# Two transformer-like blocks in one fp32 kernel: the experts' values taken from the second half on, seven pairs of split weights, and a skewed end

## The chip, the core and the metric

The program runs on one core of a Trainium2 chip. The metric is the device time of one execution in microseconds (us). TensorE (PE) does the matrix products, VectorE (DVE) and ScalarE (ACT) the elementwise work, GpSimd (POOL) a little of it, and SyncE (SP) issues the transfers, all on one queue.

## What is computed

256 tokens of width 1024 go through two blocks, all in float32. What matters here, cut from the reference:

```python
# first block
x = x + gt_mix * (concat([y_conv, y_rwkv]) @ w_out)
u = modulate(rmsnorm(x, norm_ffn_g), sh_ffn, sc_ffn)
x = x + gt_ffn * peer_ffn(u, w_q, sub_keys, expert_u, expert_v)
#   peer_ffn: per token 8 heads x top 16 of 16384 experts:
#   h = gelu(einsum('thkd,td->thk', expert_u[expert], u));  einsum('thk,thkd->td', gate * h, expert_v[expert])
x = rmsnorm(x, final_g)
# second block
h = rms_norm(x, g_mix_norm) * (1 + sc_m) + sh_m
q_a, k_a, v_a, q_i, k_i, w_i, q_b, k_b, v_b, gate_a, gate_b = split(h @ w_in)
merged = sigmoid(gate_a) * (dsa_attention(...) @ w_br_dsa) + sigmoid(gate_b) * (moba_attention(...) @ w_br_moba)
x = x + gt_m * (merged @ w_out)
h = rms_norm(x, g_ffn_norm) * (1 + sc_f) + sh_f
g_ff, u_ff = split(h @ w_gate_up)
x = x + gt_f * ((silu(g_ff) * u_ff) @ w_down)
```

The gates `gt_m` and `gt_f` are vectors over the 1024 features.

## The kernel before

**Split products.** A float32 product is made of three passes on TensorE. `wload` (L1560) loads a weight tile of 128x1024 (512 KB) into one of three raw slots (W_wraw), casts it to its high half (W_whi, on ACT or DVE) and subtracts to get the low half (W_wlo, mostly on DVE); whi and wlo have rings of three. The other operand is split as well (chi and clo, ah and al), and the passes are hi x whi, hi x wlo, lo x whi.

**The experts' values.** The gates and activations of all 16384 experts lie in SBUF as two halves, gH0 and gH1 (64 rows j of 128 experts each; 64 KB a partition). `values` (L2514) goes through the 128 rows: it splits the row's gates to ah and al (rings of three), loads the row of `peer_v`, and issues 12 matmuls of 128x512: two token tiles t x two halves of the output x three passes. For the last three rows a bias puts t=1 after t=0. Beside the rows, `beside_values` (L2576) computes the second block's modulation, and two gate rows: `row_bcast` (L1633) turns a column vector on 128 partitions x 8 into a row, by writing it to DRAM in 1024 four-byte pieces ("row<-") and reading it back onto all partitions.

**From the values to the attention.** `run` (L2869) adds the gated values to x, tile by tile (part final0 and final1: a chain of DVE and ACT steps for two norms), which ends in Cn_xn; TensorE transposes it, ACT casts it to C_chi, DVE makes C_clo. The first product is qk0 with weights w_qka, by `tok_skew` (L2329): token tile 0 goes over all 8 weights, then tile 1 over the KEEP=3 pairs that are still in the ring, and over 5 that are loaded again. Then follow the indexer, the selection, v, qk1, the gates, the attention, the merge.

**out2 and the feed-forward.** out2 is `tok_skew` over w_out_2, with a gated add (row gtm) to x, a norm, and the product "gua" (first 8 weights of gate-up, again `tok_skew`), the rest of gate-up, w_down, and a tail with the row gtf.

**What sets the order.** The program is not written in its final order. All operations are recorded (which is why the profile shows nearly everything at L696, the recorder's line), and a planner makes one fixed order for each engine and for the queue: it takes an operation's longest path to the end, adds a number from the table PRIORITY (one for a part, method and tile) and a local bias, and uses estimated costs for each operation and transfer. SBUF is divided into regions on a left and a right side (REGIONS, L1466); a region opens when the operations of the regions that it names are done. In the second block C0, Cn, Ca and Cf follow one another on the right side.

Of the kernel before, what the change touches and what calls it, by code (L numbers as in the profile page):

```python
# [205 lines left out]
def cost(op, out, reads):  # L206
    n = _free(out)
# [22 lines left out]
    if op.eng == "DMA":  # L230
        b = P * n * 4
        return b / 358.0 - 8
# [507 lines left out]
def _real(x):  # L740
# [28 lines left out]
WHI_ANY = 1  # L769
# [3 lines left out]
VAL_BIAS = 1.45e3  # L773
HALF_BIAS = 1.45e3
# [15 lines left out]
    "add C00 tensor_tensor xres": -2000.0,  # L790
    "add C01": -500.0,
    "add C01 scalar_tensor_tensor nsc": -6000.0,
    "add C01 tensor_mul gtmp": 2500.0,
    "add E00": 35000.0,
    "add E00 tensor_mul gtmp": 82500.0,
    "add E00 tensor_tensor xres": -14000.0,
    "add E01": 3500.0,
    "add E01 scalar_tensor_tensor nsc": -36000.0,
    "add E01 tensor_mul gtmp": -56000.0,
    "add E01 tensor_tensor xres": -145500.0,  # L800
    "attend00 copy ohi": -2000.0,
    "attend00 copy pT": -12000.0,
# [7 lines left out]
    "attend01 copy ohi": -2500.0,  # L810
# [6 lines left out]
    "attend01 transpose r": 500.0,  # L817
    "attend10 matmul n": -16000.0,
    "attend10 matmul p": -2000.0,
    "attend10 reciprocal asum": 1000.0,  # L820
# [5 lines left out]
    "attend11 reciprocal asum": -31000.0,  # L826
    "attend11 scalar_tensor_tensor lg1": 1000.0,
    "attend11 tensor_mul lg1": -3000.0,
    "attend11 tensor_reduce amax": 4000.0,
    "attend11 tensor_scalar amax": -2000.0,  # L830
    "attend11 tensor_sub olo": -2500.0,
    "base": 17500.0,
    "base dma_start dram": 500.0,
    "base dma_start nblk": -13500.0,
    "base memset ublk": -16000.0,
    "base tensor_mul ublkp": -57000.0,
    "base tensor_reduce ublk": 22500.0,
    "bonus matmul m": -26500.0,
    "bonus tensor_mul av": -1000.0,
    "bonus tensor_scalar av": -4000.0,  # L840
    "consts activation cvec": 40000.0,
    "consts dma_start clevf": -1500.0,
    "consts dma_start cmask": 10000.0,
    "consts dma_start cvec": -16000.0,
    "consts dma_start lorawa": 30000.0,
    "consts dma_start xres": 2000.0,
    "consts iota pj": -125500.0,
    "consts memset bd64": -43000.0,
    "consts memset bdones": -4500.0,
# [2164 lines left out]
```

## Time and profile before

| | us |
|---|---|
| median of three runs | 1500.91 (1496.61 to 1501.64) |
| the profiled execution | 1507.02 |
| its span | 1505.2 |
| TensorE busy in it | 1432.8 (95%) |
| VectorE busy | 1258.5 (84%) |
| ScalarE busy | 511.3 (34%) |

The profile is of one execution, 6 us above the median. The chain that ended last is TensorE 72%, VectorE 14%, transfers 9%, ScalarE 3%. The core's granted TensorE clock was 0.988 of full speed on the mean.

### The profile page before, as it was taken

The numbers are of one execution on the slowest core, as the hardware profiler recorded it, in microseconds if no ns is written. First come the engines' busy times: TensorE is split into PE (matmuls) and PEld (weight loads), VectorE is DVE, ScalarE is ACT, GpSimd is POOL, SyncE is SP. The second block draws the span as 40 slices with busy tenths as digits, with TensorE's granted clock in tenths as the row PEclk, the third lists the DMA queues.
The fourth block names the chain that finished last, engine by engine and source line by source line (L and its number), as shares of the span: only waits on it lengthen the run. The fifth ranks groups of instructions, "written<-read, shape, count | busy, mean of one in ns | idle before, by whom it ended". The sixth has DMA issues, their size and how long they took to land.

```text
span 1505.2 us, 24345 instructions
## 1 busy us (share of the span) xinstructions
PE 1432.8 (95%) x9307; PEld 1252.0 (83%) x9307; DVE 1258.5 (84%) x2395; ACT 511.3 (34%) x917; POOL 97.8 (6%) x91
## 2 busy tenths in 40 slices
PE   7999898998899999999999999999889999899998
PEld 6876666998899999999877888887668899589986
DVE  5798748999999889898879999887988987876676
ACT  2501225243434333232332233322354464533210
POOL 1100000023110000000000000000322100100000
PEclk9999999999999999999999999999999999999999
DMA  9558417544453545545788888786565454765554
GB/s 378 175 148 286 134 45 232 174 153 141 153 169 125 173 154 170 174 162 173 276 258 316 291 300 302 275 287 213 186 211 184 128 166 156 223 209 182 183 184 138
DMA packets 97348, 300.46 MB, mean 200 GB/s; under 512 B 17744, under 2 KB 24528, under 8 KB 97104
## 3 DMA queue, kind: packets, MB, share of 16 engines
q1 hardware_dynamic: 97232, 298.91, 60.4%
q8 instruction: 73, 1.20, 0.3%
q14 instruction: 43, 0.35, 0.1%
HBM read 295.58 MB, written 3.29 MB: 199 GB/s over the span
## 4 chain that ended last, share of the span: by engine, by line
PE 72%; DVE 14%; DMA 9%; ACT 3%; issue 2%; SPq 0%; POOL 0%; DVEq 0%; ACTq 0%; POOLq 0%
PE bank L696 72%; DVE W_wlo L696 4%; DMA W_wraw<-in_peer_v_dram 2%; ACT W_whi L696 1%; DMA W_wraw<-in_w_gua_dram 1%; DVE W_whi L696 1%; DMA row<-A_rowcol 1%; DMA Arw_XT<-scrx 1%; DMA row<-C_rowcol 1%; DVE Ach_ZR L696 1%; DMA W_wraw<-in_w_out_dram 1%; DVE Bt_tv L696 1%; DMA W_wraw<-in_peer_u_dram 1%; DVE Bt_tix L696 1%; DVE Bt_pos L696 1%
## 5 line engine op out<-in xcount | busy, mean ns | idle before, releaser
L696 DVE TENSOR_TENSOR W_wlo<-W_wraw,W_whi 128x1024 fp32r<-128x1024 f32 x417 | 515.8, 1241 | 40.4 <-ACT W_whi L696 21.8
L696 PE MATMUL bank<-X_u2hi,W_wlo 128*128 128x256 f32 x1088 | 295.4, 287 | 8.5 <-DVE W_wlo L696 8.3
L696 ACT CAST W_whi<-W_wraw 128x1024 fp32r<-128x1024 f32 x217 | 227.6, 1050 | 222.7 <-PE bank L696 128.1
L696 PE MATMUL bank<-X_u2hi,W_whi 128*128 128x256 f32 x1088 | 296.7, 287 | 3.6 <-ACT W_whi L696 2.9
L696 PE MATMUL bank<-X_u2lo,W_whi 128*128 128x256 f32 x1088 | 293.7, 285 | 0.0
L696 DVE CAST W_whi<-W_wraw 128x1024 fp32r<-128x1024 f32 x202 | 139.5, 691 | 88.2 <-PE bank L696 60.5
L696 PEld LDWEIGHTS bank<-X_u2hi,W_wlo 128*128 128x128 f32 x1088 | 202.7, 193 | 11.2 <-DVE W_wlo L696 11.1
L696 PEld LDWEIGHTS bank<-X_u2hi,W_whi 128*128 128x128 f32 x1088 | 203.1, 193 | 5.3 <-ACT W_whi L696 4.1
L696 PEld LDWEIGHTS bank<-X_u2lo,W_whi 128*128 128x128 f32 x1088 | 202.9, 193 | 0.0
L696 PE MATMUL bank<-W_whi,A_ah 128*128 128x512 f32 x512 | 139.7, 392 | 6.6 <-DVE W_whi L696 5.6
L696 PE MATMUL bank<-W_wlo,A_ah 128*128 128x512 f32 x512 | 139.9, 392 | 0.0
L696 PE MATMUL bank<-W_whi,A_al 128*128 128x512 f32 x512 | 139.2, 391 | 0.0
L696 PEld LDWEIGHTS bank<-W_whi,A_ah 128*128 128x128 f32 x512 | 96.6, 189 | 28.0 <-issue 6.8
L696 PEld LDWEIGHTS bank<-W_wlo,A_ah 128*128 128x128 f32 x512 | 96.8, 189 | 21.0 <-DVE W_wlo L696 0.9
L696 ACT CAST A_ah<-gH_gH 128x256 fp32r<-128x256 f32 x128 | 51.2, 406 | 184.1 <-PE bank L696 177.9
L696 PEld LDWEIGHTS bank<-W_whi,A_al 128*128 128x128 f32 x512 | 96.7, 189 | 20.5
L696 PE MATMUL bank<-C_chi,W_wlo 128*128 128x256 f32 (+1 forms) x424 | 108.1, 286 | 0.8 <-DVE W_wlo L696 0.7
L696 PE MATMUL bank<-C_chi,W_whi 128*128 128x256 f32 (+1 forms) x424 | 106.6, 284 | 0.0
L696 PE MATMUL bank<-C_clo,W_whi 128*128 128x256 f32 (+1 forms) x424 | 106.2, 284 | 0.0
L696 PEld LDWEIGHTS bank<-C_chi,W_wlo 128*128 128x128 f32 (+1 forms) x424 | 75.0, 188 | 1.7 <-DVE W_wlo L696 1.4
L696 DVE SCALAR_TENSOR_TENSOR A_mraw<-A_mraw,A_cvec 128x1024 f32<-128x1024 f32 x56 | 68.3, 1220 | 8.6 <-DMA A_mraw<-in_wmodT_dram 5.8
L696 PEld LDWEIGHTS bank<-C_chi,W_whi 128*128 128x128 f32 (+1 forms) x424 | 73.6, 187 | 0.8 <-ACT Ca_sg L696 0.2
(433 smaller groups left out, 2167.9 us busy)
## 6 DMA issues: line engine op xcount, KB each, us to landing
W_wraw<-in_peer_u_dram SPq DMA_DIRECT2D x128, 512.0 KB, 3.5
W_wraw<-in_peer_v_dram SPq DMA_DIRECT2D x128, 512.0 KB, 4.6
A_mraw<-in_wmodT_dram SPq DMA_DIRECT2D x48, 512.0 KB, 5.0
W_wraw<-in_w_gu_dram SPq DMA_DIRECT2D x36, 512.0 KB, 4.0
W_wraw<-in_w_down_dram SPq DMA_DIRECT2D x22, 512.0 KB, 4.3
W_wraw<-in_w_out_dram SPq DMA_DIRECT2D x17, 512.0 KB, 4.1
W_wraw<-in_w_gate_dram SPq DMA_DIRECT2D x16, 512.0 KB, 3.6
W_wraw<-in_peer_wqa_dram SPq DMA_DIRECT2D x13, 512.0 KB, 4.3
```

The lines of the kernel that those rows point to most:

```text
L696: return getattr(eng, "tensor_copy" if meth == "copy" and e != "ACT" else meth)(*args, **kw)
```

## The change

- Costs in the planner: the latency of a transfer is put at 1900 ns instead of 950, the rate at 385 bytes per ns instead of 358, and 900 ns more for scratch tensors whose names begin with "scr". The table PRIORITY is new in nearly every line (some 550 lines of the diff).
- `values` takes the rows in the order 64 to 127, 0 to 63, so that gH1 is free after 64 rows. In its room region Wx opens, with MORE=4 further pairs of whi and wlo (xhi, xlo): `wload` goes round seven pairs, three of W and four of Wx. The raw ring stays at three.
- The last LAST=7 rows have their own ring of seven for ah and al in Wx, and a bias that puts t=1 of them 9 us later.
- qk0 runs with the seven pairs and keeps all seven, and so loads one weight again instead of five. Afterwards the three pairs of W are used, until out2, where region Wf gives four more; out2 and gua load one weight again instead of five each.
- A region Cq on the right side holds what qk0 produces and the rope's temporaries. Ca opens after Wx too. The rows gtm and gtf are in Cf, which opens after Ca and Cq, instead of C0.

```diff
-DMA_LAT = 950.0
+DMA_LAT = 1900.0
     if op.eng == "DMA":
         b = P * n * 4
-        return b / 358.0 - 8
+        small = any(x.tensor.name.startswith("scr") for x in [out] + reads)
+        return b / 385.0 + (900.0 if small else 0.0)
...
 PRIORITY = {
-    "values4 tensor_tensor wlo": 14500.0,
+    "values4 matmul o": -23000.0,
...
+    "Wx": dict(side="left", after=["gH1"], on=["A3"]),
     "C0": dict(side="right", after=["Bk", "gH0", "gH1"]),
+    "Cq": dict(side="right", after=["Bk", "gH0", "gH1"], on=["C0"]),
-    "Ca": dict(side="right", after=["Cn", "A3"]),
-    "Cf": dict(side="right", after=["Ca"]),
+    "Ca": dict(side="right", after=["Cn", "A3", "Wx"]),
+    "Cf": dict(side="right", after=["Ca", "Cq"]),
+    "Wf": dict(side="left", after=["Ca", "Cq"]),
...
     def wload(self, ap, n=1024):
+        self.turn = (self.turn + 1) % (3 + MORE) if self.more else 0
         raw = self.T("W", "wraw", [1024], F32, WRAW)[:, 0:n]
         nc.sync.dma_start(raw, ap)
-        hi = self.T("W", "whi", [1024], F32R, 3)[:, 0:n]
-        (nc.any.copy if WHI_ANY else nc.scalar.copy)(hi, raw)
-        lo = self.T("W", "wlo", [1024], F32R, 3)[:, 0:n]
+        more = self.turn >= 3
+        hi = self.T(self.more, "xhi", [1024], F32R, MORE)[:, 0:n] if more else self.T("W", "whi", [1024], F32R, 3)[:, 0:n]
+        nc.any.copy(hi, raw)
+        lo = self.T(self.more, "xlo", [1024], F32R, MORE)[:, 0:n] if more else self.T("W", "wlo", [1024], F32R, 3)[:, 0:n]
...
 def tok_skew(net, hi, lo, aps, tag):
+    keep = KEEP + MORE if net.more else KEEP
-    tok_mm(net, hi, lo, aps, ps, order_back(0), (1,), kept=kept)
+    tok_mm(net, hi, lo, aps, ps, order_back(keep), (1,), kept=kept, keep=keep)
...
     def values(self, side):
-        for j in range(128):
+        for n in range(128):
+            j = (n + 64) % 128
+            last = n >= 128 - LAST
+            if n == 64:
+                net.more = "Wx"
+            part = lambda x: net.T("Wx", x + "x", [32, 8], F32R, LAST) if last else net.T("A3", x, [32, 8], F32R, 3)
-                        nc.bias = -VAL_BIAS * (2 * t + h) if j >= 125 else 0.0
+                        nc.bias = -VAL_LATE * t - VAL_BIAS * h if last else 0.0
...
     def run(self, peer_ps, out):
+        net.more = "Wf"
-        gtm = net.row_bcast("C0", 1, 2, "row", 2, scale=0.5)
+        gtm = net.row_bcast("Cf", 1, 2, "row", 2, scale=0.5)
...
-        gtf = net.row_bcast("C0", 1, 5, "row", 2)
+        gtf = net.row_bcast("Cf", 1, 5, "row", 2)
```

TensorE at the end of the values and the start of qk0, before: bank_61 and bank_60 are tile 0's output, bank_62 and bank_63 tile 1's, A_ah and A_al a row's split gates, W_whi and W_wlo its split values.

```order
L696 MATMUL bank_62<-W_whi_85,A_ah_6965 128x512
L696 MATMUL bank_62<-W_wlo_88,A_ah_6965 128x512
L696 MATMUL bank_62<-W_whi_85,A_al_6968 128x512
L696 MATMUL bank_63<-W_whi_85,A_ah_6965 128x512
L696 MATMUL bank_63<-W_wlo_88,A_ah_6965 128x512
L696 MATMUL bank_63<-W_whi_85,A_al_6968 128x512
L696 MATMUL bank_64<-G_ident_74,Cn_xn_9305 128x128 x4
L696 MATMUL bank_65<-G_ident_74,Cn_xn_9306 128x128 x4
```

Before, the last 18 matmuls of tile 1 stand between tile 0's last one and the transposes (the last row of tile 1 is shown). After, bank_63 and bank_62 are tile 0's, bank_61 and bank_60 tile 1's:

```order
L697 MATMUL bank_62<-W_whi_86,Wx_alx_8151 128x512
L697 MATMUL bank_61<-W_whi_85,Wx_ahx_8138 128x512
L697 MATMUL bank_61<-W_wlo_88,Wx_ahx_8138 128x512
L697 MATMUL bank_61<-W_whi_85,Wx_alx_8145 128x512
L697 MATMUL bank_60<-W_whi_85,Wx_ahx_8138 128x512
L697 MATMUL bank_60<-W_wlo_88,Wx_ahx_8138 128x512
L697 MATMUL bank_60<-W_whi_85,Wx_alx_8145 128x512
...
L697 MATMUL bank_60<-W_whi_86,Wx_ahx_8144 128x512
L697 MATMUL bank_60<-W_wlo_89,Wx_ahx_8144 128x512
L697 MATMUL bank_60<-W_whi_86,Wx_alx_8151 128x512
L697 MATMUL bank_65<-G_ident_74,Cn_xn_9248 128x128 x4
L697 MATMUL bank_64<-G_ident_74,Cn_xn_9249 128x128 x4
```

Now 42 matmuls of tile 1, those of the last seven rows, stand there (the first six and the last three are shown).

The queue (SP) at the end of the values, before: C_rowcol is the column of gtm, C_row its row.

```order
L696 DMA C_rope_9273<-in_rope_dram 128x384
L696 DMA C_causal_9275<-in_causal_dram 128x128
L696 DMA row<-C_rowcol_9294 128x8x1
L696 DMA C_row_9295<-row 128x1024
L696 DMA C_row_9296<-row 128x1024
L696 DMA W_wraw_82<-in_w_qka_dram 128x1024
L696 DMA W_wraw_83<-in_w_qka_dram 128x1024
L696 DMA W_wraw_84<-in_w_qka_dram 128x1024
```

The queue in out2, after (Cf_rowcol and Cf_row the same column and rows):

```order
L697 DMA W_wraw_82<-in_w_out_dram 128x1024
L697 DMA W_wraw_84<-in_w_out_dram 128x1024
L697 DMA row<-Cf_rowcol_11064 128x8x1
L697 DMA W_wraw_83<-in_w_out_dram 128x1024
L697 DMA Cf_row_11065<-row 128x1024
L697 DMA W_wraw_82<-in_w_out_dram 128x1024
L697 DMA W_wraw_84<-in_w_out_dram 128x1024
L697 DMA Cf_row_11066<-row 128x1024
L697 DMA W_wraw_83<-in_w_out_dram 128x1024
L697 DMA W_wraw_82<-in_w_gua_dram 128x1024
```

The scatter has moved from the front of the qk0 loads to between the fifth and the sixth load of w_out; its read-back stands before the last three loads.

VectorE in out2, after: the end of the merge (Ca_mg), then the column, and the splits of out2's weights (the third to sixth of its eight).

```order
L697 SCALAR_TENSOR_TENSOR Ca_mg_0_9708<-Ca_sg_9694,bank_63 128x512
L697 TENSOR_TENSOR Ca_mg_9707<-Ca_mg_9707,Ca_mg_0_9708 128x512
L697 TENSOR_TENSOR C_clo_9215<-Ca_mg_9707,C_chi_9214 128x512
L697 TENSOR_SCALAR Cf_rowcol_11064<-G_mod_78 128x8
L697 CAST Wf_xhi_11103<-W_wraw_83 128x1024
L697 SCALAR_TENSOR_TENSOR Cf_nsc_11069<-G_mod_78,G_cols_72 128x8
L697 TENSOR_TENSOR Wf_xlo_11107<-W_wraw_83,Wf_xhi_11103 128x1024
L697 TENSOR_TENSOR Wf_xlo_11108<-W_wraw_82,Wf_xhi_11104 128x1024
L697 TENSOR_TENSOR Wf_xlo_11109<-W_wraw_84,Wf_xhi_11105 128x1024
L697 CAST Wf_xhi_11106<-W_wraw_83 128x1024
L697 TENSOR_TENSOR Wf_xlo_11110<-W_wraw_83,Wf_xhi_11106 128x1024
```

The column stands right behind the merge's last operations, ahead of the splits of the third to sixth weight.

## Rows read from the trace of the kernel before

**Rows 1.** The page's busy times: busy us, share of the span, instructions.

```profile
PE 1432.8 (95%) x9307; PEld 1252.0 (83%) x9307; DVE 1258.5 (84%) x2395; ACT 511.3 (34%) x917; POOL 97.8 (6%) x91
```

**Rows 2.** The page's costliest group: busy us, mean ns, idle before.

```profile
L696 DVE TENSOR_TENSOR W_wlo<-W_wraw,W_whi 128x1024 fp32r<-128x1024 f32 x417 | 515.8, 1241 | 40.4 <-ACT W_whi L696 21.8
```

**Rows 3.** Stretches: us; busy of PE, PEld, DVE, ACT, POOL; clock; DMA share, GB/s.

```profile
0.00:420.00 420.00, 379.37 (x2586) 318.40 (x2587) 340.80 (x931) 138.98 (x223) 46.50 (x53) 0.98 0.55 182
860.00:1000.00 140.00, 140.00 (x620) 115.83 (x619) 124.85 (x182) 48.89 (x78) 0.00 (x0) 1.00 0.86 295
1060.30:1118.30 58.00, 47.66 (x193) 35.35 (x192) 50.08 (x86) 26.80 (x53) 20.03 (x20) 0.94 0.58 188
1273.10:1332.80 59.70, 52.83 (x214) 36.24 (x213) 50.84 (x70) 30.98 (x48) 4.57 (x3) 1.00 0.70 218
```

**Rows 4.** TensorE's timeline, end of values and qk0: start, us, [idle before].

```profile
1083.74 1.67 PE L696 MATMUL bank<-G_ident,Cn_xn 128*128 128x128 f32 x8 [4.22 <-DVE Cn_xn L696]
1087.26 1.22 PE L696 MATMUL bank<-W_whi,C_chi 128*128 128x512 f32 x2 [1.85 <-ACT C_chi L696]
...
1091.51 0.63 PE L696 MATMUL bank<-W_whi,C_clo 128*128 128x512 f32 x2
1091.98 0.63 PE L696 MATMUL bank<-W_whi,C_chi 128*128 128x512 f32 x2
...
1095.94 0.73 PE L696 MATMUL bank<-W_wlo,C_chi 128*128 128x512 f32 x2 [0.54 <-DVE W_wlo L696]
...
1099.60 1.11 PE L696 MATMUL bank<-G_ident,Cn_xn 128*128 128x128 f32 x8 [1.06 <-DVE Cn_xn L696]
```

**Rows 5.** VectorE's timeline at the same place.

```profile
1074.31 0.69 DVE L696 TENSOR_TENSOR A_mraw<-bank,A_gtf 128x512 f32<-128x512 f32 x1 [0.52 <-PE bank L696]
...
1083.14 1.15 DVE L696 TENSOR_SCALAR Cn_xn<-A_mraw,A_f2r,A_f2t 128x512 f32<-128x512 f32 x2
```

**Rows 6.** The queue's timeline at the same place.

```profile
1074.66 0.43 SPq L696 DMA_DIRECT2D row<-C_rowcol  x1
1086.36 0.80 SPq L696 DMA_DIRECT2D C_row<-row  x2
```

**Rows 7.** Transfers, 160 to 185 and 770 to 790: KB, us to landing.

```profile
row<-G_mod SPq DMA_DIRECT2D x1, 4.0 KB, 9.2
...
row<-A_rowcol SPq DMA_DIRECT2D x1, 4.0 KB, 12.0
```

**Rows 8.** Timelines of the queue, VectorE and TensorE around the values' two scatters.

```profile
772.05 0.33 SPq L696 DMA_DIRECT2D W_wraw<-in_peer_v_dram  x1
772.43 0.43 SPq L696 DMA_DIRECT2D row<-A_rowcol  x1
...
783.93 0.69 DVE L696 CAST W_whi<-W_wraw 128x1024 fp32r<-128x1024 f32 x1 [4.85 <-DMA W_wraw<-in_peer_v_dram]
...
1049.61 0.69 DVE L696 CAST W_whi<-W_wraw 128x1024 fp32r<-128x1024 f32 x1 [7.64 <-DMA W_wraw<-in_peer_v_dram]
...
1058.78 0.69 DVE L696 CAST W_whi<-W_wraw 128x1024 fp32r<-128x1024 f32 x1
...
1061.00 0.69 DVE L696 CAST W_whi<-W_wraw 128x1024 fp32r<-128x1024 f32 x1
...
1050.44 2.04 PE L696 MATMUL bank<-W_whi,A_ah 128*128 128x512 f32 x4 [2.52 <-DVE W_whi L696]
1052.29 1.75 PE L696 MATMUL bank<-W_wlo,A_ah 128*128 128x512 f32 x4
```

**Rows 9.** TensorE's waits in out2 and gua: in total, times, longest.

```profile
PE bank L696 <- DVE W_wlo L696: 3.5, 7, 0.7
```

**Rows 10.** The page's issues: KB each, median us to landing.

```profile
W_wraw<-in_w_out_dram SPq DMA_DIRECT2D x17, 512.0 KB, 4.1
```

**Rows 11.** Timelines of the queue and of TensorE in the first block.

```profile
163.73 1.03 SPq L696 DMA_DIRECT2D row<-G_mod  x1
...
176.39 1.06 PE L696 MATMUL bank<-G_ident,Arw_XT 128*128 128x128 f32 x4 [3.40 <-DMA Arw_XT<-scrx]
```

More of the change, by code (lines that the diff above doesn't have):

```diff
@@ L768 @@
 CONV32 = True
-WHI_ANY = 1
+MORE = 4
 PREP_BIAS = 10e3
@@ L1062 @@
-    "mats3 copy_predicated XT": -46000.0,
-    "mats3 dma_start XT": -30500.0,
-    "mats3 matmul b": -56500.0,
-    "mats3 transpose b": -4000.0,
+    "index tensor_tensor wlo": -1000.0,
+    "index transpose r": -18500.0,
+    "mats0": -4000.0,
+    "mats0 copy WT": 20000.0,
+    "mats0 copy X": -11500.0,
+    "mats0 copy Ylev": -15000.0,
+    "mats0 copy_predicated X": 11500.0,
+    "mats0 copy_predicated XT": -4000.0,
+    "mats0 dma_start XT": 18000.0,
+    "mats0 matmul a": -34000.0,
+    "mats0 transpose a": 10000.0,
@@ new lines @@
+    "mats1": -5000.0,
+    "mats1 copy WT": -32000.0,
+    "mats1 copy Ylev": 16500.0,
+    "mats1 copy_predicated X": 10500.0,
+    "mats1 copy_predicated XT": -17500.0,
+    "mats1 dma_start XT": -30000.0,
+    "mats1 matmul b": -1000.0,
+    "mats1 transpose b": 2500.0,
+    "mats2": 500.0,
+    "mats2 copy WT": -15000.0,
+    "mats2 copy X": 27000.0,
+    "mats2 copy Ylev": -15000.0,
+    "mats2 copy_predicated X": -71500.0,
+    "mats2 copy_predicated XT": 16000.0,
+    "mats2 dma_start XT": -70000.0,
@@ L1066 @@
+    "mats2 matmul a": 6000.0,
+    "mats2 transpose a": 500.0,
+    "mats3": 8500.0,
+    "mats3 copy X": 9000.0,
+    "mats3 copy Ylev": 6000.0,
+    "mats3 copy_predicated X": -1000.0,
+    "mats3 copy_predicated XT": -36000.0,
+    "mats3 dma_start XT": -500.0,
+    "mats3 matmul b": -20500.0,
+    "mats3 transpose b": 2000.0,
     "merge": -1000.0,
@@ L1199 @@
+    "out0 matmul v": -3000.0,
     "out1": 1000.0,
-    "out1 matmul v": 500.0,
-    "out2": -12000.0,
-    "out2 dma_start dram": -16500.0,
-    "out2 dma_start row": 16000.0,
+    "out1 matmul v": -7500.0,
+    "out2": -14000.0,
+    "out2 dma_start dram": -14500.0,
+    "out2 dma_start row": 20000.0,
     "out2 tensor_scalar rowcol": 16000.0,
     "out20": -15000.0,
-    "out20 dma_start wraw": -17000.0,
+    "out20 dma_start wraw": -29000.0,
     "out20 matmul o": 8000.0,
-    "out20 tensor_tensor wlo": 4000.0,
+    "out20 tensor_tensor wlo": 8000.0,
@@ L1369 @@
     "sums3": -6000.0,
+    "sums3 matmul g": 18000.0,
+    "sums3 tensor_mul gH1": 2500.0,
     "sums3 tensor_tensor oj": 500.0,
-    "tail": 67000.0,
+    "tail": 83000.0,
     "tail dma_start dram": 2000.0,
-    "tail tensor_mul outt": -8000.0,
+    "tail tensor_mul outt": 24000.0,
     "tail tensor_tensor outt": -1000.0,
@@ L1418 @@
     "values0 dma_start wraw": 33000.0,
-    "values0 matmul o": 4000.0,
     "values0 tensor_sub al": -2000.0,
-    "values0 tensor_tensor wlo": -1000.0,
+    "values0 tensor_tensor wlo": 1000.0,
     "values1": 1000.0,
@@ L1523, in load_consts @@
         self.ring = 0
+        self.more, self.turn = None, 0
         nc.bias = 2 * FIRST_BIAS
@@ L2314, in tok_mm @@
     for n, k in enumerate(ks):
-        w[k] = whi, wlo = kept[k] if kept and n < KEEP else net.wload(aps[k])
+        w[k] = whi, wlo = kept[k] if kept and n < keep else net.wload(aps[k])
         for t in tt:
```

799 lines of the change are left out of this document (403 added, 396 removed).

## The prediction

> **What bounds the kernel now.** I read the page's busy times first: TensorE is busy 1432.8 of 1505.2 us, VectorE 1258.5, of which 515.8 make the low halves of weights (wlo, 1.24 us each) [rows 1, 2]. TensorE therefore idles about 72 us in all, and because both kernels issue the same matmuls, a change of order can only win or lose inside these 72 us. A table of stretches then says where they lie [rows 3]. The first block up to 420 us holds 420 - 379.4 = 40.6 us of idling, an undisturbed stretch of the values none (140.0 busy of 140.0). The stretch from 84 matmuls before the end of the values to the end of qk0 holds 10.3, and out2 with gua 6.9. The last two are where the change puts its extra pairs, so I read TensorE's timeline there, then the two queues that feed it.
>
> At the end of the values, TensorE stops for 4.22 us for the normalized values (xn) and 1.85 for their split, restarts slowly (two 512-wide matmuls take 1.22 us, against 0.63 later), and waits for single weights and for token tile 1's xn inside qk0 [rows 4]. VectorE's chain for xn begins when tile 0's last bank is done, at 1074.31, and reaches xn at 1083.14 [rows 5]. Beside it a transfer of 1024 four-byte pieces (a row scattered to DRAM) is issued at 1074.66, and the row's read-back, which waits for it, at 1086.36 [rows 6]. There are four such scatters, and they took 9.2, 9.7, 11.7 and 12.0 us to land, though each moves 4 KB (the shortest and the longest: [rows 7]). Loads around one wait as well: the weight load issued at 772.05, just ahead of a scatter, was cast only at 783.93, and behind the second in the values VectorE stood 7.64 us for a raw weight and TensorE 2.52 for its cast [rows 8]. In out2 and gua the waits are many and short, for wlo above all, and 192 matmuls and their transposes take 59.7 us [rows 3, 9].
>
> **The end of the values and qk0.** A 512-wide matmul here takes 0.235 us (groups of two start 0.47 us apart, at 1091.51 and 1091.98, [rows 4]). Before, three rows' token tile 1 came after tile 0: 18 matmuls, 4.1 us, lay over VectorE's chain. Now seven rows' do: 42 matmuls, 9.5 us. The chain from tile 0's bank to xn is 1083.74 - 1074.31 = 9.4 us, so the stop of 4.22 goes, less some 1 for splits of weights that the new order puts between (each 1.24 us). The split of xn is still waited for, 1.85. The slow restart cost some 1.9 (ten matmuls from 1087.26 to 1091.51, at 0.425 instead of 0.235, [rows 4]) and should mostly go with the long stop. In qk0 four reloads vanish, and with them three waits of about half a us, of which the last is shown (0.54). Against this, tile 1's chain now starts 5.4 us later against the end of tile 0, and I add 2.8 us to its wait of 1.06 before the second group of transposes; the scatter and its two reads no longer stand before the qk0 loads. Sum: 4.2 - 1 + 1.9 + 1.4 - 2.8 + about 2 for smaller waits = 6 gained (bounds 0 and 9: nothing of the waits goes; all of the listed ones but 1.85 do).
>
> **out2 and gua.** Eight reloads vanish (four each), some 8 x 1.24 + 4 x 0.69 = 13 us of VectorE's work, in a stretch where it is busy 50.8 of 59.7 [rows 3]. With three pairs TensorE's waits for wlo alone are 3.5 us [rows 9]. But the gate row's scatter, which stood at the end of the values, now stands between the fifth and sixth w_out load, and the queue then halts for its read-back. With X the start of out2 on TensorE: the scatter can go at about X+3.7 (after four vector operations that end the merge), the sixth weight lands at about X+15 and is cast by X+16; TensorE, with 45 matmuls before it, is there at X+11 and stops for 5 to 6 us. The seventh load is issued only when the scatter has landed, is usable at about X+22, and costs another 2.5. A restart such as the one behind the stop of 2.52 us (matmul groups of 2.04 and 1.75 for 1.07, [rows 8]) adds 1.7. Then: 192 x 0.235 = 45.0, transposes 2.7, the stop 8.5, slow 1.7, the split of xn 1.9 (as at qk0), the gated add 1, small gaps 1: 61.8 against 59.7, or 2 lost. Best case: the scatter lands like a load in 4 us (the nearest row, 4.1 for w_out, [rows 10]) and nothing stops: about 50.5, 9 gained. Worst: the load ahead of the scatter is caught too, as the one at 772.05 was; TensorE then stops at matmul 32, X+7.5, until about X+16.5, and out2 with gua takes some 66: 7 lost. I take -2, because all four scatters measured lie at 9 to 12.
>
> The Trainium skill (DMA: Bandwidth & Descriptors, Anatomy of one DMA) counts a transfer at a fixed 2.0 us plus bytes over 436 GB/s, by which the 4 KB row would land in 2 us and out2 would gain the 9 of the best case. The same page's rules for kernel authors say that a strided last dimension lowers to one descriptor per element, and this rule speaks against the change; the trace agrees with it (9.2 to 12.0 us). The first rule's result is rival (a) below; neither enters the sum.
>
> **Values.** Rows are taken in the order 64 to 127, 0 to 63; the cost of a row is the same. From the 64th on seven pairs are there, but the split of the gates (ah, al) still has a ring of three on the same VectorE queue, so VectorE can't run far ahead. The first scatter comes before that and costs what it did. The second comes at row 118, seven to ten rows before the end, and its 2.52 us stop plus slow rows of 1.7 may shrink: +1 (0 to 4).
>
> **The first block.** The table is new in every stage. The first row's scatter moves ahead of four w_out loads and of both reads of scrx, of which the later was waited for 3.40 us [rows 11]; the reads then stand behind the scatter, and what the later one gains the earlier can lose. Nothing in the trace prices the rest: the order is different on every engine, and the idle time is 40.6. I take +1, bounds -5 and +5, an eighth of that idling either way. Start, index to merge, gate-up, w_down and the tail: 0, since TensorE has almost no idle time to give there and its work is unchanged.
>
> **Sum.** 6 - 2 + 1 + 1 = 6 us gained. The profiled execution took 1507.0 us (span 1505.2), so it would take 1501.0. The median of the three runs, 1500.9, is 6.1 lower; in its terms the time is 1495.
>
> **Rivals.**
> (a) The scatter in out2 lands quickly or is hidden, and the extra pairs pay in full: 11 more than in the sum, 1484. For it: no other transfer of scratch data stands beside it there, and out2's queue is quieter than the values'. Against it: the one at 1074.66, with only small tables beside it, still took until 1086. 0.13.
> (b) The two skews cancel: tile 1's chain on VectorE gives back more than 2.8 in qk0 (gain of 3 there instead of 6), and out2 loses 5: 3 - 5 + 1 + 1 = 0, 1501. For it: VectorE is busy 50.1 of 58 us at that place, and busy engines don't shorten a wait. Against it: fewer reloads there. 0.26.
> (c) Slower: the first pass of a skew asks for splits faster than VectorE makes them. Six matmuls a weight are 1.36 to 1.41 us; VectorE's pitch near the values' end is 2.2 us a row (its casts at 1058.78 and 1061.00 are a row apart, [rows 8]). Entering the pass with no pair ahead, it is 7 x (2.2 - 1.4) = 5.6 late; this eats the 6 at the values' end, and in out2, where the scatter takes the lead away, the loss is 7: 0 - 7 + 0 + 1 = -6, 1507. It decides from fewer than three pairs ahead on (four rows then need 8.8 of 9.5 us). For it: the second scatter, with 7.64 us of VectorE standing still, falls about ten rows before the pass. Against it: seven pairs, and VectorE at 124.9 of 140 us in the values, which leaves 11% to run ahead. 0.17.
> (d) My forecast: 0.44.
>
> **How the numbers follow.** About 0.3%, 4.5 us, is what a measurement of this kernel can tell from no change. Faster by more: nearly all of (a), three quarters of the forecast and a little of (b): 0.13 + 0.34 + 0.07 = 0.54. Slower by more: most of (c) and a tenth of (b) and of the forecast's spread on the first block: 0.19. The rest, 0.27, is the same. The forecast's own range, from the first block's 5 and out2's bounds in part, is 1488 to 1502. For eight in ten the range reaches to (a) and to (c) with its own spread: 1480 to 1508.
>
> **What would show it.** Right: in the changed profile no stop over 2 us ahead of qk0's transposes, the stretch of 58.0 us at about 52; in out2 one stop of 4 to 8 us for a cast or for a w_out load, with a scatter that takes 9 or more to land before it; w_qka, w_gua with 9 loads. Wrong: a scatter that lands in out2 without a stop (then a), TensorE waiting for Wx pairs in the 42 matmuls of tile 0 (then c), or a first block whose length differs by more than 5 us, which would outweigh everything worked out here.

## The result, and the profile after

The changed kernel takes 1508.5 us (median of six runs, 1502.5 to 1511.9) against 1500.7 for the kernel before: a ratio of 1.0052 [1.0032, 1.0071], slower by half a per cent. The forecast was 1495, and faster.

The page's first row after (busy us, share of the span, instructions; the span is 1510.1):

```profile
PE 1432.2 (95%) x9307; PEld 1252.5 (83%) x9307; DVE 1227.4 (81%) x2365; ACT 511.5 (34%) x923; POOL 100.3 (7%) x91
```

TensorE's busy time is what it was [rows 1], and VectorE has 31 us less to do. Of the low halves [rows 2] 404 are made instead of 417:

```profile
L697 DVE TENSOR_TENSOR W_wlo<-W_wraw,W_whi 128x1024 fp32r<-128x1024 f32 x319 | 397.2, 1254 | 20.8 <-ACT W_whi L697 14.3
...
L697 DVE TENSOR_TENSOR Wf_xlo<-W_wraw,Wf_xhi 128x1024 fp32r<-128x1024 f32 x44 | 53.3, 1224 | 6.6 <-ACT Wf_xhi L697 3.7
```

(the other 41 go to Wx_xlo). So the extra pairs do save the reloads, and the time still rose. The stretches that answer to [rows 3], after (the second line here starts 82 matmuls before the values' end and holds 191 instructions of TensorE; the third is out2 and gua):

```profile
0.00:420.00 420.00, 378.08 (x2585) 316.88 (x2586) 331.82 (x926) 132.24 (x215) 47.46 (x54) 0.97 0.54 183
...
1071.90:1119.80 47.90, 44.16 (x191) 34.97 (x190) 37.57 (x69) 19.68 (x43) 19.28 (x20) 0.93 0.44 159
1276.40:1340.80 64.40, 50.22 (x212) 38.23 (x211) 42.34 (x63) 25.80 (x42) 3.37 (x2) 0.95 0.52 173
```

58.0 became 47.9 for two instructions fewer; over the same 193 it is 58.3 and 48.6 (fifteen of them are now matmuls of 128x256, worth 1.7 us, so some 8 are gained for equal work). 59.7 became 64.4. To account for the whole, I cut TensorE's timeline of each run's one profiled execution at the same instructions: the first matmul of the values, the last one, the first of out2, the last of gua, and TensorE's last matmul (4.5 us before the end of the span, so the sums are shorter than the spans; that before's sum equals its median is chance). All runs stand here; those below the second line are the experiments. The ratio is to the kernel before timed beside the run, whose median was 1499.7 to 1502.4.

| us | to the values | values | to out2 | out2, gua | rest | sum | median | ratio |
|---|---|---|---|---|---|---|---|---|
| before | 720.8 | 358.8 | 193.6 | 59.9 | 167.8 | 1500.7 | 1500.7 | 1 |
| after | 728.7 | 363.1 | 184.6 | 64.4 | 164.8 | 1505.6 | 1508.5 | 1.0052 |
| front_old | 718.9 | 360.0 | 183.9 | 65.3 | 164.8 | 1492.9 | 1503.3 | 1.0020 |
| front_new | 728.4 | 365.6 | 201.4 | 63.1 | 166.5 | 1525.0 | 1531.3 | 1.0199 |
| wx_shift32 | 724.2 | 359.1 | 183.2 | 64.4 | 165.9 | 1496.7 | 1506.1 | 1.0046 |
| wx_shift288 | 722.1 | 359.2 | 183.0 | 64.6 | 164.8 | 1493.7 | 1507.8 | 1.0045 |
| before_shift96 | 719.7 | 356.7 | 190.0 | 58.5 | 165.9 | 1490.8 | 1497.4 | 0.9991 |
| row_flat | 730.3 | 361.9 | 183.0 | 54.4 | 165.1 | 1494.6 | 1498.6 | 0.9984 |
| both_fixed | 718.1 | 367.0 | 183.2 | 64.2 | 164.4 | 1496.8 | 1501.0 | 1.0008 |
| rows_by_pe | 712.3 | 354.7 | 182.2 | 53.3 | 164.4 | 1466.9 | 1476.8 | 0.9846 |
| before_rows | 713.4 | 349.1 | 189.5 | 58.5 | 165.0 | 1475.5 | 1482.5 | 0.9874 |
| rows_noskew | 715.0 | 350.1 | 184.1 | 53.9 | 165.6 | 1468.6 | 1477.6 | 0.9848 |
| rows_nowf | 712.1 | 356.1 | 181.6 | 66.6 | 170.3 | 1486.6 | 1491.1 | 0.9925 |
| after_rows | 723.5 | 357.4 | 182.4 | 55.1 | 164.3 | 1482.6 | 1483.0 | 0.9873 |

The second line against the first: -7.9 (front), -4.4 (values), +9.0, -4.6 (out2 and gua), +3.0, together 4.9 lost; the medians differ by 7.8. One execution is no median: before's profiled one lies 6.3 above the median and after's 3.4, and single executions of one order differ by up to 8 us in a column (722.1 to 730.3 in the first). Columns are trusted below where several kernels share the order.

**The end of the values.** TensorE's timeline after, which answers to [rows 4]:

```profile
1091.41 0.40 PE L697 MATMUL bank<-W_whi,Wx_alx 128*128 128x512 f32 x1
1091.65 1.04 PE L697 MATMUL bank<-G_ident,Cn_xn 128*128 128x128 f32 x8
1095.26 0.73 PE L697 MATMUL bank<-W_whi,C_chi 128*128 128x512 f32 x2 [2.58 <-ACT C_chi L697]
...
1097.08 1.22 PE L697 MATMUL bank<-W_whi,C_clo 128*128 128x512 f32 x2 [0.56 <-DVE C_clo L697]
1098.10 1.06 PE L697 MATMUL bank<-Wx_xhi,C_chi 128*128 128x512 f32 x2
...
1105.97 0.39 PE L697 MATMUL bank<-W_whi,C_chi 128*128 128x512 f32 x1
1106.20 1.04 PE L697 MATMUL bank<-G_ident,Cn_xn 128*128 128x128 f32 x8
```

The transposes follow the last value matmul without a stop; the 4.22 us is gone, and so is tile 1's 1.06. The wait for the split has grown from 1.85 to 2.58, and the slow restart stays: from 1097.10 to 1103.10 the granted clock is 0.50 of full speed, its lower level (1.2 GHz), behind the stops of 2.58 and 0.56, and fourteen 512-wide matmuls take 0.43 us each (two of them 1.06 from 1098.10 on). Before, ten did.

**out2.** TensorE, VectorE and the queue after, and the transfers of 1270 to 1300 (KB, us to landing):

```profile
1286.66 0.40 PE L697 MATMUL bank<-Wf_xlo,C_chi 128*128 128x512 f32 x1
1294.70 1.22 PE L697 MATMUL bank<-Wf_xhi,C_chi 128*128 128x512 f32 x2 [7.65 <-DVE Wf_xhi L697]
...
1293.96 0.69 DVE L697 CAST Wf_xhi<-W_wraw 128x1024 fp32r<-128x1024 f32 x1 [10.35 <-DMA W_wraw<-in_w_out_dram]
...
1279.51 0.38 SPq L697 DMA_DIRECT2D row<-Cf_rowcol  x1
1281.37 0.33 SPq L697 DMA_DIRECT2D W_wraw<-in_w_out_dram  x1
1290.88 0.33 SPq L697 DMA_DIRECT2D Cf_row<-row  x1
```

```profile
W_wraw<-in_w_out_dram SPq DMA_DIRECT2D x7, 512.0 KB, 6.8
...
row<-Cf_rowcol SPq DMA_DIRECT2D x1, 4.0 KB, 11.3
```

Out2 starts at X = 1276.4; the scatter goes at X+3.1 and lands 11.3 us later. The sixth weight, issued right behind it at 1281.37, is cast at X+17.5, and TensorE has stood since X+10.7. That load took 12.6 us to land; in the 11.3 us of the scatter the DMA engines moved 21 GB/s.

**The first block.** TensorE after, in the query product of the first block (from the first matmul with X_u2hi, at 236.10, on; the other wait is 0.53), then the stretch behind its first stops and 93 instructions of that product as one stretch (columns as in [rows 3]):

```profile
244.90 0.73 PE L697 MATMUL bank<-W_whi,X_u2hi 128*128 128x512 f32 x2 [1.49 <-DVE W_whi L697]
...
249.57 0.48 PE L697 MATMUL bank<-G_ident,E_xn 128*128 128x128 f32 x1 [0.62 <-POOL E_xn L697]
...
253.70 0.93 PE L697 MATMUL bank<-G_ident,E_xn 128*128 128x128 f32 x7
...
257.46 0.50 PE L697 MATMUL bank<-W_whi,X_u2hi 128*128 128x512 f32 x1 [1.45 <-ACT X_u2hi L697]
```

```profile
246.16:253.20 7.04, 6.42 (x15) 4.60 (x16) 5.09 (x8) 1.34 (x2) 3.43 (x2) 0.52 0.66 228
236.10:265.80 29.70, 25.61 (x93) 19.42 (x94) 21.72 (x32) 12.63 (x21) 4.14 (x3) 0.83 0.55 194
```

The same 93 instructions before, and the wait that answers to the 1.45:

```profile
234.40:259.30 24.90, 22.71 (x93) 17.48 (x93) 19.41 (x29) 14.11 (x23) 2.15 (x2) 0.93 0.74 241
...
250.03 0.73 PE L696 MATMUL bank<-W_whi,X_u2hi 128*128 128x512 f32 x2 [0.95 <-ACT X_u2hi L696]
```

They take 29.7 us instead of 24.9. The second token tile's eight transposes stand otherwise in TensorE's order: one, and the other seven only 4.1 us later. What hangs on them (VectorE's and ScalarE's scaling, then the split X_u2hi) is late with them, but TensorE waits only 0.5 longer for it (1.45 against 0.95). More is lost elsewhere: the stop of 1.49 for a weight's cast is new, and behind it the granted clock falls to 0.52 of full speed, the lower level (1.2 GHz), from 246.16 to 253.20, where 512-wide matmuls take 0.43 us instead of 0.23. Waits make up some 1.9 of the 4.8 us, and matmuls at the lower clock some 2.4. The granted clock over the whole stretch is 0.83, before 0.93. It isn't the clock alone: in the runs front_new and wx_shift32 below, which have the same order of TensorE here, these instructions took 26.8 and 27.1 us at 0.94 (and 28.1 and 29.1 at 0.88 in wx_shift288 and row_flat), against 24.6 to 25.0 in four executions of the old order.

### The profile page after: what moved, and what is told of

The parts are those of the page before. It is cut to its first block, busy times and chain, and to the rows that moved or that the text cites. A ratio compares the mean times of both kernels' runs of the same rounds, so it can differ in the third digit from the quotient of the medians.

```text
span 1510.1 us, 24221 instructions
## 1 busy us (share of the span) xinstructions
PE 1432.2 (95%) x9307; PEld 1252.5 (83%) x9307; DVE 1227.4 (81%) x2365; ACT 511.5 (34%) x923; POOL 100.3 (7%) x91
## 4 chain that ended last, share of the span: by engine, by line
PE 65%; DVE 17%; DMA 11%; issue 3%; ACT 2%; SPq 0%; POOL 0%; POOLq 0%; DVEq 0%; ACTq 0%
PE bank L697 65%; DVE W_wlo L697 5%; DMA A_mraw<-in_wmodT_dram 3%; DMA W_wraw<-in_peer_v_dram 2%; DVE W_whi L697 1%; DMA Afeat_hraw<-in_adaR_dram 1%; DMA row<-A_rowcol 1%; DMA row<-Cf_rowcol 1%; DVE Bt_pos L697 1%; DMA Arw_XT<-scrx 1%; DVE Bt_tix L697 1%; DVE A_al L697 1%; ACT W_whi L697 1%; DMA An_mraw<-in_adaT_dram 1%; DVE Bt_best L697 1%
## 5 line engine op out<-in xcount | busy, mean ns | idle before, releaser
L697 DVE TENSOR_TENSOR W_wlo<-W_wraw,W_whi 128x1024 fp32r<-128x1024 f32 x319 | 397.2, 1254 | 20.8 <-ACT W_whi L697 14.3
L697 DVE CAST W_whi<-W_wraw 128x1024 fp32r<-128x1024 f32 (+1 forms) x134 | 93.1, 696 | 71.9 <-PE bank L697 41.7
L697 PE MATMUL bank<-W_wlo,A_ah 128*128 128x512 f32 x356 | 97.0, 395 | 1.8 <-DVE W_wlo L697 1.7
L697 PE MATMUL bank<-W_whi,A_ah 128*128 128x512 f32 x356 | 95.7, 391 | 3.0 <-ACT W_whi L697 1.8
L697 PE MATMUL bank<-W_whi,A_al 128*128 128x512 f32 x356 | 96.5, 393 | 1.0 <-DVE A_al L697 0.8
L697 DVE SCALAR_TENSOR_TENSOR A_mraw<-A_mraw,A_cvec 128x1024 f32<-128x1024 f32 x56 | 68.4, 1221 | 17.7 <-DMA A_mraw<-in_wmodT_dram 13.8
L697 PEld LDWEIGHTS bank<-W_wlo,A_ah 128*128 128x128 f32 x356 | 66.6, 189 | 18.4 <-DVE W_wlo L697 4.9
L697 PE MATMUL bank<-C_chi,W_wlo 128*128 128x256 f32 (+1 forms) x256 | 67.7, 286 | 1.0 <-DVE W_wlo L697 1.0
L697 PE MATMUL bank<-C_chi,W_whi 128*128 128x256 f32 (+1 forms) x256 | 67.8, 285 | 0.0
L697 PE MATMUL bank<-C_clo,W_whi 128*128 128x256 f32 (+1 forms) x256 | 67.6, 285 | 0.0
L697 DVE TENSOR_TENSOR Wf_xlo<-W_wraw,Wf_xhi 128x1024 fp32r<-128x1024 f32 x44 | 53.3, 1224 | 6.6 <-ACT Wf_xhi L697 3.7
L697 DVE TENSOR_TENSOR A_al<-gH_gH,A_ah 128x256 fp32r<-128x256 f32 x121 | 50.5, 420 | 2.9 <-ACT A_ah L697 2.1
```

The source lines that it names most:

```text
L697: return getattr(eng, "tensor_copy" if meth == "copy" and e != "ACT" else meth)(*args, **kw)
```

## The experiments

All kernels are timed beside the kernel before, and the figure in brackets is the 95% interval of the ratio; the table has the stretches. "Theory" and "rival" stand in the expectations.

**Where the first block's part of the loss is.** `front_old` is the changed kernel with the costs and table entries of the kernel before for the parts of the first block alone, so that TensorE's first block is row for row that of before and the queue from the values on is that of after (TensorE's order there is the same but for 202 of 3996 places).

```diff
+def _late(part): ...          # parts of the second block, the values and what stands beside them
-        return b / 385.0 + (900.0 if small else 0.0)
+        return b / 385.0 + (900.0 if small else 0.0) if _late(op.part) else b / 358.0 - 8
```

> The changed kernel, with the kernel before's costs and PRIORITY lines for the parts of the first block only; its first block is row for row that of the kernel before, its queue from the values on that of the changed kernel. Theory (first block loses some 8): values start at about 721, time 1508.5 - 8 = 1500 to 1502. Rival (second half loses): time stays at 1507 to 1509.

1503.3, 1.0020 [1.0006, 1.0033]; the front is 718.9. `front_new` turns it round: the kernel before, with the changed costs and the changed table entries for the first block.

```diff
-DMA_LAT = 950.0
+DMA_LAT = 1900.0
...
 PRIORITY = {   # the first block's entries from the changed table, the others as before
```

> The kernel before, with the changed kernel's planner costs and its PRIORITY lines for the parts of the first block (up to the hidden stage); its first block is then row for row that of the changed kernel. Theory (the retuned first block loses the time: in the two traces the values start at 720.8 and 728.7): values start about 8 us later than in the kernel before, time 1506 to 1510. Rival (the loss is in the second half, the two first blocks differ by chance): values start within 2 us of the kernel before's, time about 1501.

1531.3, 1.0199 [1.0177, 1.0222]. It can't be read as a measure of the front: the new costs, without the entries that go with them, also re-planned the second block (201.4 to out2). The expectation of 1506 to 1510 was missed for that reason. But its front alone, 728.4, agrees. Over all kernels with the rows scattered as before, the old order of the first block gives 718.1 to 720.8 (four), the new one 722.1 to 730.3 (five). The means, 719.4 and 726.7, are 7.4 apart; in time, front_old is some 5 us (0.32%) better than the changed kernel.

**Why the values became slower.** In after, the twelve matmuls of a row had two speeds. Start, us, in the middle of the values:

```profile
954.82 1.07 PE L697 MATMUL bank<-W_whi,A_ah 128*128 128x512 f32 x4
955.73 1.07 PE L697 MATMUL bank<-W_wlo,A_ah 128*128 128x512 f32 x4
...
961.27 1.10 PE L697 MATMUL bank<-Wx_xlo,A_ah 128*128 128x512 f32 x4
962.21 1.10 PE L697 MATMUL bank<-Wx_xhi,A_al 128*128 128x512 f32 x4
```

Four start 0.91 us apart with a pair in W and 0.94 with a pair in Wx (0.227 and 0.233 a matmul on the mean). The shapes are the same; what differs is where the tiles lie. I shifted region Wx by 32 bytes, and by 288.

```diff
+            if r == "Wx":
+                pools[r].tile([P, 32], U8, name="Wx_first")   # and 288 in the other
```

> The changed kernel, with 32 unused bytes at the start of region Wx, so that its tiles' addresses leave the same rest (96) as those of the split gates when divided by 256, but not by 512; the order is unchanged. In the changed kernel a 512-wide matmul of the values takes 0.2267 us where the moving tile lies in W and 0.2333 where it lies in Wx. Theory (what counts is the difference of the two operands' addresses within some power of two of at most 256): 0.2267 for Wx too, 3 us faster than the changed kernel. Rival (within 512, or the place of Wx in itself): 0.2333 as before, same time.

> As the run with 32 bytes, but 288, so that the rests agree for 512 as well (352). Theory (a difference within 512 or less counts): 0.2267 us for the matmuls with a moving tile in Wx, about 430 of them, 430 x 0.0066 = 2.9 us less. Rival (Wx is slow wherever it lies, as the far side of SBUF or because of what is written there): 0.2333, same time.

Both remove it (wx_shift32):

```profile
948.60 1.07 PE L699 MATMUL bank<-Wx_xhi,A_ah 128*128 128x512 f32 x4
949.51 1.07 PE L699 MATMUL bank<-Wx_xlo,A_ah 128*128 128x512 f32 x4
950.42 1.07 PE L699 MATMUL bank<-Wx_xhi,A_al 128*128 128x512 f32 x4
```

0.91 apart, as in W, and the values take 359.1 and 359.2 instead of 363.1. That both shifts, 256 apart, do the same fits a rule on the rest of the address modulo 256, and speaks against the place of Wx in itself. The times, 1.0046 and 1.0045, are not told apart from 1.0052 (1.0032 to 1.0071), so the 3 us that were expected are shown in the pitch and not in the time: 430 slower matmuls cost about 2.5 us, less than these runs resolve. The same holds before the change: qk0's 512-wide matmuls of W_whi with C_chi started 0.47 us apart in twos [rows 4]. `before_shift96` shifts what lies behind C0 by 96 bytes.

```diff
+            if r == "C0":
+                pools[r].tile([P, 96], U8, name="C0_last")
```

> The kernel before with 96 unused bytes in region C0, in the same order: the tiles chi, clo, fhi and flo (held by TensorE while W moves) then leave the same rest as W's tiles when divided by 256 (96 for 192 before). Theory (rests that differ cost 0.0066 us a matmul): 792 matmuls of the second block go from 0.2345 to 0.2275 us, 5.2 us faster, 1500 to 1495; where TensorE waits for splits anyway, less. Rival (the second block's 0.2345 comes from the order, two matmuls to a held tile of a token tile, not from addresses): pitch and time unchanged. Its profile is also a second one of the order of the kernel before: the run of before that was profiled lay 7 above the median, and the theory is that it lost them after the values' start (780 us there; 773 expected here).

```profile
1125.83 0.62 PE L698 MATMUL bank<-W_whi,C_chi 128*128 128x512 f32 x2
1126.29 0.63 PE L698 MATMUL bank<-W_wlo,C_chi 128*128 128x512 f32 x2
1126.76 0.62 PE L698 MATMUL bank<-W_whi,C_clo 128*128 128x512 f32 x2
1127.21 0.61 PE L698 MATMUL bank<-W_whi,C_chi 128*128 128x512 f32 x2
```

0.46 apart now (1.38 over three, against 1.41 before). In time 0.9991 [0.9980, 1.0003]: at most 0.2%, not certainly anything, where 5.2 us were expected; where the rest of TensorE's saving goes is not shown.

**What the scatter costs in out2.** `row_flat` leaves everything in place and only changes how the 4 KB of gtm's row go to DRAM: in 128 pieces of 32 bytes instead of 1024 of four. Its row has the features in another order, so the output is not the reference's.

```diff
-        nc.sync.dma_start(scratch_ap(row, [[1, P], [P, 8]]), col)
+        nc.sync.dma_start(scratch_ap(row, [[8, P], [1, 8]] if which == 1 and i == 2 else [[1, P], [P, 8]]), col)
```

> The changed kernel, in the same order, with the scatter of the gate row gtm written as 128 pieces of 32 bytes instead of 1024 of 4 (the row's features then stand in another order, so the output is not the reference's). Theory (the scatter holds the loads of out2): the stop of 7.65 us in out2 is under 1, out2 with gua takes 55 to 57 instead of 64.4, time 1500 instead of 1508. Rival (out2 waits for splits and for the loads' places in the queue, whatever the scatter takes): a stop of 5 or more stays, time within 2 of the changed kernel's.

The transfers of 1270 to 1300, and the longest wait in TensorE's timeline of its out2 and gua:

```profile
W_wraw<-in_w_out_dram SPq DMA_DIRECT2D x6, 512.0 KB, 4.7
...
row<-Cf_rowcol SPq DMA_DIRECT2D x1, 4.0 KB, 1.4
```

```profile
1300.74 0.72 PE L697 MATMUL bank<-Wf_xhi,C_chi 128*128 128x512 f32 x2 [1.79 <-ACT C_chi L697]
```

The row lands in 1.4 us instead of 11.3, and the load behind it in 4.6 instead of 12.6. The stop of 7.65 is gone (waits of 1.35, 0.76, 1.21 and 0.52 remain in gua), and out2 with gua takes 54.4 instead of 64.4. The time is 1498.6, 0.9984 [0.9967, 1.0001], ten us under the changed kernel. This one transfer turns the change from slower to not slower. The Trainium skill (DMA: Bandwidth & Descriptors, Anatomy of one DMA) gives a transfer a fixed 2.0 us plus its bytes, measured on transfers that GpSimd issues. Here SyncE issues them, and 1.4 us for 128 pieces and 11.3 for 1024 of the same 4 KB show that here the pieces set it. The Trainium skill's rule on the same page (Rules for kernel authors), one descriptor per element for a strided last dimension, agrees: the trace of row_flat has 1024 packets of 4 bytes fewer than that of after, and 128 of 32 bytes. Whether their number or their size counts, no run separates.

**Both repaired, the scatter left.** `both_fixed` is front_old with Wx shifted by 32 bytes and C0's end by 128.

> The changed kernel with the first block's order of the kernel before (as in front_old) and with the addresses of Wx, chi, clo, fhi and flo shifted to W's rest (32 and 128 unused bytes). Theory (both effects are separate and add): front_old's 1503 less 2.9 for Wx and less 5 for the second block, 1495 to 1496. Rival (the time that TensorE saves is waited for again, VectorE being nearly full): 1501 to 1503.

1501.0, 1.0008 [0.9992, 1.0025]: no change against before, as the rival had it. Front and pitch no longer lose, and what the values' end wins is lost again in out2 (4.3) and, in the profiled execution, in the values (8.2). That execution also shows what a scatter in the values can do:

```profile
780.17 2.07 PE L715 MATMUL bank<-W_wlo,A_ah 128*128 128x512 f32 x4 [5.42 <-DVE W_wlo L715]
```

**No scatters at all.** `rows_by_pe` goes on from both_fixed: the column [128 x 8] is turned on TensorE, and written in 8 pieces of 512 bytes. All four rows are made so, and a bias is to put them ahead of what else can be done. Region G holds the turned rows, which is why the shifts are others. The rows also go at other times: the second is written at 906.8 instead of 768.3, and gtm's at 1221 instead of 1271.3. So this run changes the pieces and the place of the transfers together.

```diff
-        nc.sync.dma_start(scratch_ap(row, [[1, P], [P, 8]]), col)
+        pt = self.psum("r")
+        nc.tensor.transpose(pt[0:8, 0:P], col, self.ident[:])
+        turned = self.T("G", "rowt", [P], F32, 2)
+        nc.scalar.copy(turned[0:8, :], pt[0:8, 0:P])
+        nc.sync.dma_start(scratch_ap(row, [[P, 8], [1, P]]), turned[0:8, :])
```

> As both_fixed, with each of the four gate rows turned on TensorE and written as 8 pieces of 512 bytes instead of scattered as 1024 of 4. Theory (the scatters hold the queue): the two stops in the values go (5 and 4 us with their slow restarts), out2 with gua takes 54 to 57 instead of 64: 15 less than both_fixed, about 1480. Rival (the scatters' stops are replaced by waits for splits): 1490 to 1495.

The busy row, the landing times of those transfers of a row for which the trace has one (three that read a row back; the four that write one have none), and TensorE's waits in out2 and gua (in total, times, longest):

```profile
PE 1413.7 (96%) x9311; PEld 1244.9 (85%) x9311; DVE 1225.0 (83%) x2362; ACT 517.0 (35%) x931; POOL 92.7 (6%) x90
```

```profile
DMA to landing us min/median/max: 3.3/5.3/6.2
```

```profile
PE bank L715 <- DVE Wf_xlo L715: 1.4, 1, 1.4
PE bank L715 <- ACT C_chi L715: 1.2, 1, 1.2
PE bank L715 <- POOL Cf_xn L715: 1.2, 1, 1.2
PE bank L715 <- DVE W_wlo L715: 0.8, 1, 0.8
```

1476.8, 0.9846 [0.9826, 0.9866], the best of all runs: 24 us under both_fixed, where 15 were expected. So how much of this is the change, and how much the rows? `before_rows` is the kernel before with the same four rows and shifts of regions, and none of the change.

> The kernel before (three pairs, its own tables) with the four gate rows turned on TensorE and the addresses shifted, that is with both cures of rows_by_pe and nothing of the change. Theory (seven pairs, the seven-row skew and the order after them are worth 8 us between the values' end and out2 and 5 in out2 with gua): 1476.8 + 13 = about 1490. Rival (once the scatters are gone the pairs pay nothing): 1476 to 1480.

1482.5, 0.9874 [0.9847, 0.9900]. Most is the rows: 19 us, of which before_shift96 allows the shift some 1. Seven pairs, skews and all give 0.28% more (0.9846 against 0.9874, with intervals that overlap), far less than the expectation. By stretches they win 7.3 to out2 and 5.2 in out2, and lose 5.6 in the values of that one execution. Two more executions with the same order up to the last rows took 350.1 (rows_noskew) and 356.1 (rows_nowf), against 349.1 in before_rows; TensorE waits 3.3, 1.0 and 4.8 us there with seven pairs and 0.1 with three, for the split gates above all. So the loss is 1 to 7 us in the three, and its cause was not settled. `after_rows` is the changed kernel with the rows alone, its first block and Wx as they are.

> The changed kernel with the four rows turned on TensorE and nothing else (new first block, addresses of Wx and chi as they fall). Theory (what the scatters cost is separate): 10 in out2 as in row_flat and 5 to 8 in the values less, 1508 - 16 = 1492; the matmuls with a moving tile in Wx still at 0.2333 us. Rival (only out2's counts): 1498.

1483.0, 0.9873 [0.9837, 0.9909], with a front of 723.5, 10 us more than before_rows; the rows don't heal the first block. The time is 9 us below the expectation, so the scatters cost this kernel more than the theory said. Set beside before_rows (0.9874), it is the plainest answer on the change: with the scatters gone from both, the changed kernel and the kernel before take the same time (the latter with the addresses shifted as well, which is worth some 1 us).

**Pairs or skew.** `rows_noskew` is rows_by_pe, with only the last three rows in the order t=0, then t=1.

```diff
-            nc.bias = -VAL_LATE * t - VAL_BIAS * h if last else 0.0
+            nc.bias = -VAL_BIAS * (2 * t + h) if n >= 128 - SKEW else 0.0   # SKEW = 3
```

> rows_by_pe with only the last three rows' token tile 1 put behind tile 0, as before; the seven pairs stay in the values' second half, qk0, out2 and gua. Theory (the skew covers the wait for xn): the 4 us stop ahead of qk0 is back, 1480 to 1482. Rival (the pairs alone do it): 1476 to 1478.

```profile
1065.76 1.11 PE L715 MATMUL bank<-G_ident,Cn_xn 128*128 128x128 f32 x8 [0.72 <-DVE Cn_xn L715]
...
1070.22 1.22 PE L715 MATMUL bank<-W_whi,C_chi 128*128 128x512 f32 x2 [3.35 <-ACT C_chi L715]
```

1477.6, 0.9848 [0.9818, 0.9878], the same as rows_by_pe. The theory that the long skew covers VectorE's chain falls: with three rows the wait for xn is 0.72, not the 4.22 of [rows 4]. In rows_by_pe only the 2.11 for chi stands there, so the skew of seven is worth about 2 us in waits. That gtm's scatter no longer stands there doesn't explain it either, for with the scatters gone and three pairs the stop is as long as ever (before_rows):

```profile
1066.89 1.37 PE L698 MATMUL bank<-G_ident,Cn_xn 128*128 128x128 f32 x8 [4.35 <-DVE Cn_xn L698]
```

What shortens the stretch is the seven pairs with the order made for them, which no run separates.

`rows_nowf` leaves region Wf unused from out2 on (three pairs, as before the change).

```diff
-        net.more = "Wf"
+        net.more = None
```

> rows_by_pe with three pairs from out2 on (region Wf unused). Theory (reloads and their splits hold out2 and gua): that stretch goes from 53.3 to 58 or 59 us, the rest by 1 longer, 1483. Rival (it was bound by something else): 1476 to 1478.

```profile
PE bank L715 <- DVE W_wlo L715: 7.0, 10, 1.8
PE bank L715 <- ACT C_chi L715: 3.0, 2, 2.0
PE bank L715 <- DVE W_whi L715: 2.0, 2, 1.5
```

1491.1, 0.9925 [0.9896, 0.9954]: 66.6 in out2 and gua where 58 or 59 was expected, and 5.9 more in the rest. In a table that was made for seven pairs, the pairs from out2 on are worth 12 us by the ratios; against before_rows, whose table was made for three, 5 to 6 (53.3 and 58.5, 164.4 and 165.0).

## Why the prediction was wrong

**The first block is the step that failed.** It was put as "I take +1, bounds -5 and +5", while the text before it said that nothing prices it. It measures -7.4 over nine executions, beyond its bound. The text's own reading (the scatter ahead of both reads of scrx, gain and loss cancelling) gives the smaller part. At TensorE's last transposes of Afeat_modrows (159.1 us) both kernels are level; the read's wait grew from 3.40 [rows 11] to 5.17, and 1.7 us in all are lost from there to the query product. In it 4.8 are lost, in waits and in matmuls at the lower clock behind them (1.9 to 4.2 in the four other executions with this order), and behind it 1.4 (a stage of 0.4 less, one of 1.8 more). That seven of eight transposes of the second tile stand behind more matmuls could have been read from the order of TensorE, but they are worth 0.5 us of wait; the larger one is the 1.49 for a weight's cast, which itself had waited 0.97 for its load. front_old shows that the first block was lost in its order: with the old order its front is 718.9, and the time some 5 us shorter. Why the hidden activations behind it take 280.2 to 280.7 instead of 278.4 in every kernel with the new order was not settled.

**"Can only win or lose inside these 72 us" was wrong too.** TensorE's idle time doesn't bound a loss, and it didn't bound a gain: rows_by_pe's span is 33.8 us shorter than before's, and 19.1 of that is busy time (1413.7 against 1432.8). Busy time also holds the matmuls at the lower clock behind a stop and those of the slower pitch; the mean granted clock is 0.995 there, and 0.988 before.

**The values: "the cost of a row is the same" was wrong.** +1 became -4.4. TensorE's waits there are the same in sum (6.5 us and 6.6 before), and the 2.52 behind the second scatter did go, as forecast. The loss is in part the pitch of matmuls on Wx, 0.006 a matmul, some 2.5 us for 430; about 2 us are within the spread of single executions.

**The values' end and qk0: mechanism right, size too small.** 6 (0 to 9) became some 8 in the stretch the prediction named (58.3 to 50.3 for equal work), and 9.0 up to out2; against before_shift96, which has less to lose there, 5.4. The stop of 4.22 went, as did the three reload waits; tile 1's wait of 1.06, to which 2.8 was added for VectorE's later chain, fell to none. The 1.9 of the slow restart did not go: fourteen matmuls took 0.43 us, ten before. But the long skew, to which the prediction gave the credit, is worth 2 us; three rows and seven pairs do nearly the same.

**out2 and gua: mechanism right, -2 became -4.6, inside its bounds (+9 to -7).** The scatter went at X+3.1 (X+3.7 was said) and the sixth weight was cast at X+17.5 (X+16); the stop was 7.65 (5 to 6), the next 0.60 (2.5), together 8.25 against 8.5. What was under-sized is the rest: waits of 1.36, 0.75, 1.20 and 0.53 in gua, where the sum had 1 for gaps (nearly the same four stand in row_flat, so the scatter isn't their cause). The term of the scatter is confirmed at the size: row_flat gains 10.0 with it gone.

**The tail: 0 became +3.0** against the profile, but 1.1 against before_shift96; before's 167.8 is the longest of all but rows_nowf.

**The rivals.** (a) fell: the scatter wasn't hidden; row_flat, where the row landed in 1.4 us, comes near it in out2 (54.4, the best case being about 50.5) but not in time (1498.6, not 1484). (b), a cancelling of skews, was near in out2 (5 lost, 4.6 measured) and fell at qk0 (3 gained, 9). (c) had the number, 1507, but not the mechanism: in the last 42 matmuls of tile 0, the first pass that it spoke of, TensorE waits once, 0.60 us for a W_wlo, where it had 5.6. The loss was made in a place that no rival named. The prediction had set it as a point where it would be wrong ("a first block whose length differs by more than 5 us"), and gave it no case of its own.

## What to carry to other kernels

When a change replaces a planner's costs and table, the re-planned stages far from its aim need a price of their own: compare the order at the few places where the trace of before waits, and give the loss a rival of its own. Look at transfers by pieces, not bytes: with four rows of 4 KB turned on TensorE first, instead of written in four-byte pieces, three kernels here took some 19 to 27 us less, more than everything the change was about (the rows were written at other times too; row_flat, which changes one row's pieces alone, gained 10). A gain that rests on a queue's spare time should be tried with the slow transfer on that queue taken away, before buffers are added around it.

## What was not expected of the hardware

- A 512-wide fp32r matmul takes 0.227 or 0.232 to 0.234 us, by where its moving and its held tile lie. Shifts of Wx by 32 and by 288 bytes, and of what lies behind C0 by 96 (before_shift96) or 128 (both_fixed), made the slow pairs fast. By the layout of these kernels the two addresses then agree modulo 256 bytes; that nothing but this rest counts is inferred from these four shifts. No such difference was seen for 128x256 matmuls. Why, no run here tells.
- A scatter of 1024 four-byte pieces holds back the load that is issued behind it on the same queue: in after the one of 1281.37 took 12.6 us to land and served a cast only at 1293.96, where row_flat's, behind 128 pieces of 32 bytes, took 4.6.
- In the first block, too, the rows cost something: to the values 713 us without the scatter (means of four executions) and 719 with it, in nearly the same order of the rest.
